# A hybrid encoder layer on one core: the B gates spread over the q, k pairs, W_c directly behind z, and one maximum tile for two heads

## The chip, the core and the metric

The kernel runs on one core of one Trainium2 chip. The metric is the time of one execution on the device, in microseconds (us), as the median of several runs. TensorE (PE, with its weight loads as PEld) does the products and the transposes, ScalarE (ACT) and VectorE (DVE) split the operands and do everything elementwise, GpSimd (POOL) does one addition per SSD head, and SyncE (SP) issues the loads of the weights. TensorE runs at one of two clock levels, 1.2 or 2.4 GHz, which the profile reports as a granted clock of 0.5 or 1.0.

## The reference

There are two layers (DEPTH 2) over 256 positions of width 1024, in float32. In each layer one combined projection of u = RMSNorm(x) feeds three branches and their gates:

```
u = RMSNorm(x);  proj = u @ w_in  ->  conv A | q, k, v | z | x, B, C of the SSD | dt | g_A, g_B, g_C
y_A = W_A (B * conv3(C * x_A))
y_B = W_B (dilated attention of q, k, v: 16 heads of 64, softmax over a mask of counts)
y_C = W_C (GroupRMSNorm((SSD_fwd + SSD_bwd + D x) * silu(z)))     4 groups of 512 channels
x = x + W_o (sig(g_A) y_A + sig(g_B) y_B + sig(g_C) y_C)
x = x + W_2 relu(W_1 RMSNorm(x))^2
```

Behind the second layer stands a final RMSNorm. What matters here: y_B needs all 16 heads, y_C needs z, the SSD output and the mean square of each group of 512 channels, and a gate needs only u.

## The kernel before, in words

Every product is done in three float32r matmuls: each operand is split into a high part and a rest (`split_to`, L172: a cast on ACT at L173, a subtraction on DVE at L174), and high by high, high by rest and rest by high are added in PSUM. I call these three matmuls a triplet. The weights come as tiles of 128 x 1024 in the order in which they are used (`Stream`, L150; the order is `_weight_stream`, L886). The raw tile has 4 buffers, its two parts `wh` and `wl` have 3 each.

Two forms of product occur. `chunks` (L189) gives the output with channels on the partitions: a weight tile is 8 triplets of 256 columns, and a q, k pair is two such tiles (L181 to L184). `wide` (L229) gives the output with positions on the partitions: one weight tile is 4 triplets of 512 columns, done as two steps of 2 triplets, one for each half of the positions (t = 0, 1), with two PSUM banks open until its last step (L248 to L250). With `lag=1`, as for W_c, the second half runs one tile behind the first. There are 4 PSUM banks for products (`mm`), two for scores (`s`), one for transposes (`pt`) and one for attention and SSD outputs (`oy`).

Two things set the order. TensorE's program is written out: `Slots` counts ticks, one for every 4 triplets of `chunks` and for every step of `wide`, and a job that was launched with a delay places its own matmuls when its tick comes. The other engines' programs are ordered at build time by a scheduler from priorities; at run time each engine goes through its own list in order and waits where an operand isn't there.

Around the change a layer goes: gate A, W_a, then eight q, k pairs (L694 to L702), gate B with its eight weight tiles (L711), the wait for all attention (L713), W_b, four groups of z (L734 to L744) with a `group_norm` job each (L720), gate C (L745), a wait for the fourth group's norm (L747), W_c (L779), W_o.

- `attention` (L638) is launched 5 ticks after its pair, for two heads. It places four score matmuls (tile `s`, L644); DVE adds the mask and takes maxima (L653), scales them (L655), ACT does the exponentials (L657) with sums, DVE the reciprocals (L659), ACT the scaling (L661, tile `scr`). Five ticks after the scores come the transposes of the first head (tile `pt`, L668), two ticks later those of the second, then the product with v (L682).
- `ssd_pair` (L520) does two SSD heads: sums on POOL (L531) and DVE (L532), exponentials on ACT (L534, L538), two DVE products (L542, L543), then the output matmuls (L552). `ssd_job` (L559) holds new pairs back between the first q, k pair and the sixth attention.
- `group_norm` waits GN_DELAY ticks behind its group of z, sums squares over channels with a matmul (tile `sqa`, L288), waits GN_DELAY2 ticks, spreads the factor over the partitions with another matmul (tile `pt`, from `rs`, L303), and scales and splits four channel tiles (L730, then L173 and L174 to `ch` and `cl`). The fourth group has a raised priority.
- A tile that takes 8 KB of a partition (`big`, L137) has one of 11 buffers; a twelfth waits until one is free.

Of the kernel before, what the change touches and what calls it, by code (L numbers as in the profile page):

```python
# [11 lines left out]
F32 = mybir.dt.float32  # L12
# [6 lines left out]
P = 128  # L19
# [25 lines left out]
Y_DELAY = 6  # L45
SSD_RESUME = 5
SSD_START = 4
GN_DELAY = 9, 9
GN_DELAY2 = 6, 5


def _bits(v, n):
# [36 lines left out]
def trunk_kernel(ctx: ExitStack, tc: tile.TileContext, xT, pos, wst, wdt, small, fin, consts, out):  # L89
# [136 lines left out]
                    tick()  # L226
        return ps

    def wide(st, r, sink, lag=0):  # L229

        rows = sum(h.shape[1] for h, _ in r)
        per = r[0][0].shape[1]
        for c in range(2):
            ps = [mmbank(), mmbank()]
            n = rows // 2
            ws = {}
            order = [(i, t) for i in range(n) for t in range(2)]
            for i, t in sorted(order, key=lambda a: (a[0] + lag * a[1], a[1])):  # L240
                if t == 0:
                    ws[i] = [t_.rearrange("p (k c) -> p k c", k=2) for t_ in st.next()]
                wh, wl = ws[i] if t == 0 else ws.pop(i)
                us = slice(t * 128, t * 128 + 128)
                for k in range(2):
                    kt = 2 * i + k
                    rh, rl = (t_[:, kt % per, us] for t_ in r[kt // per])
                    PE.matmul(ps[t], rh, wh[:, k, :], start=kt == 0, stop=False)  # L248
                    PE.matmul(ps[t], rh, wl[:, k, :], start=False, stop=False)  # L249
                    PE.matmul(ps[t], rl, wh[:, k, :], start=False, stop=kt == rows - 1)  # L250
                if i == n - 1:
                    sink(t, c, ps[t])
                tick()

    def half(tile_, t, c):

        v_ = tile_.rearrange("p a b -> p (a b)").rearrange("p (t c) -> p t c", t=2)
        return v_[:, t, c * 512 : c * 512 + 512]
# [129 lines left out]
    def layer(l, xw, squares):  # L388
# [131 lines left out]
        def ssd_pair(g, hp, xt, cb, ar, crs):  # L520
            bs = ssd["bs"]
            ct = 4 * g + hp
            av = []
            for j in range(2):
                h = 2 * ct + j
# [98 lines left out]
        mix = big("mix", F32)  # L624

        def gate(dst):
            wide(st, [u], lambda t, c, ps: ACT.activation(half(dst, t, c), ps, AF.Tanh, scale=0.5))

        ga = big("ga", F32)
        gate(ga)  # L630
        wide(st, [(ah, al)], lambda t, c, ps: DVE.scalar_tensor_tensor(
            half(mix, t, c), half(ga, t, c), 1.0, ps, ALU.add, ALU.mult))
        bh, bl = big("bh"), big("bl")
# [4 lines left out]
        def attention(c, qk):  # L638
            scs, prts = [], []
            sps = [bank("s", 2), bank("s", 2)]  # L640
            for t in range(2):
                for j in range(2):
                    rows = slice(j * 64, j * 64 + 64)
                    PE.matmul(sps[j][:, t * 256 : t * 256 + 256], qk[rows, 0, t * 128 : t * 128 + 128],  # L644
                              qk[rows, 1, :], start=True, stop=True)
            for j, sp in enumerate(sps):
                sc = scr[:, (2 * c + j) % 4]
                scs.append(sc)
                mx = tmp.tile([P, 2], F32, name="mx", bufs=4)
                den = tmp.tile([P, 2], F32, name="den", bufs=4)  # L650
                rden = tmp.tile([P, 2], F32, name="rden", bufs=4)
                for t in range(2):
                    DVE.tensor_tensor_reduce(sc[:, t, :], sp[:, t * 256 : t * 256 + 256], cntm[:, t, :],  # L653
                                             1.0, -3.0e38, ALU.add, ALU.max, mx[:, t : t + 1])
                DVE.tensor_scalar(mx, mx, -0.125, None, ALU.mult)  # L655
                for t in range(2):
                    ACT.activation(sc[:, t, :], sc[:, t, :], AF.Exp, bias=mx[:, t : t + 1], scale=0.125,  # L657
                                   accum_out=den[:, t : t + 1])
                DVE.reciprocal(rden, den)  # L659
                for t in range(2):  # L660
                    ACT.activation(sc[:, t, :], sc[:, t, :], AF.Copy, scale=rden[:, t : t + 1])  # L661
            yield 2
            yield 3
            for j in range(2):
# [26 lines left out]
        done.add("qk")  # L691
        cosb = cosT.unsqueeze(1).to_broadcast([P, 2, 256])
        sinb = sinT.unsqueeze(1).to_broadcast([P, 2, 256])
        for c in range(8):  # L694
            psv = chunks(st, 2, u)
            qk = tmp.tile([P, 2, 256], F32, name="qk", bufs=2)
# [3 lines left out]
            DVE.tensor_tensor(sw, sw, sinb, ALU.mult)  # L700
            DVE.tensor_tensor(qk, qk, sw, ALU.add)
            slots.launch(attention(c, qk), ATT_DELAY)  # L702

        def gated_add(g_):
            def sink(t, c, ps):
# [2 lines left out]
                DVE.tensor_tensor(m, m, th, ALU.add)  # L708
            return sink

        gb = big("gb", F32)  # L711
        gate(gb)
        slots.until(lambda: "attention" in done)  # L713
        wide(st, [(bh, bl)], gated_add(gb))

# [18 lines left out]
        for g in range(4):  # L734
# [7 lines left out]
                DVE.tensor_tensor(xq, xq, sz, ALU.mult)  # L742
                sq.add(xq)
            slots.launch(group_norm(g, xg, sq), GN_DELAY[g == 3])  # L744
        gc = big("gc", F32)  # L745
        gate(gc)
        slots.until(lambda: ("norm", 3) in done)  # L747

        mh, ml = big("mh"), big("ml")
        mixv = mix.rearrange("p a b -> p (a b)").rearrange("p (t c) -> p t c", t=2)  # L750
# [25 lines left out]
            if t == 1 and c == 0:  # L776
                slots.launch(turn_job(0), 6)

        wide(st, [(ch[0], cl[0]), (ch[1], cl[1])], c_sink, 1)  # L779


        xm = Pairs("xm", 2)
# [103 lines left out]
def _weight_stream(w_in, w_a, w_b, w_c, w_o, w1, w2, last):  # L886
    seq = []
# [5 lines left out]
    for g in range(4):  # L893
        seq += [xb[16 + g], xb[20 + g], ab[2 * g], ab[2 * g + 1]]
        seq += [xb[4 * g], xb[4 * g + 1], ab[8 + 2 * g], ab[9 + 2 * g]]
        seq += [xb[4 * g + 2], xb[4 * g + 3], ab[16 + 2 * g], ab[17 + 2 * g]]
    seq += _wide(w_in[:, og : og + 1024]) + _wide(w_a)
    for c in range(8):
        seq += [inb[oq][c], inb[oq][8 + c]]
    seq += _wide(w_in[:, og + 1024 : og + 2048]) + _wide(w_b)  # L900
    seq += list(inb[oz]) + _wide(w_in[:, og + 2048 : og + 3072]) + _wide(w_c)
    for w in (w_o, w1) + (() if last else (w2,)):
        wb = _blocks(w)
        for c in range(wb.shape[0]):
# [85 lines left out]
```

## Time and profile before

| | us |
|---|---|
| median of 3 runs (1377.03, 1384.38, 1382.09) | 1382.09 |
| the profiled execution's own time | 1378.66 |
| its span from first to last instruction | 1376.9 |
| PE busy in the span | 1351.1 (98%) |
| DVE busy | 1034.3 (75%) |
| ACT busy | 877.0 (64%) |
| mean granted clock of TensorE | 0.998 |

Busy time is a sum over the span. Matmuls are pipelined, so that the starts of two in a row, not their durations, tell how fast TensorE goes. The last column of a wait is the longest single one. Of one layer's stretches only the ones that the change touches are shown below; the second layer repeats the first some 680 us later.

### The profile page before, as it was taken

The numbers are of one execution on the slowest core, as the hardware profiler recorded it, in microseconds if no ns is written. First come the engines' busy times: TensorE is split into PE (matmuls) and PEld (weight loads), VectorE is DVE, ScalarE is ACT, GpSimd is POOL, SyncE is SP. The second block draws the span as 40 slices with busy tenths as digits, with TensorE's granted clock in tenths as the row PEclk, the third lists the DMA queues.
The fourth block names the chain that finished last, engine by engine and source line by source line (L and its number), as shares of the span: only waits on it lengthen the run. The fifth ranks groups of instructions, "written<-read, shape, count | busy, mean of one in ns | idle before, by whom it ended". The sixth has DMA issues, their size and how long they took to land.

```text
span 1376.9 us, 22642 instructions
## 1 busy us (share of the span) xinstructions
PE 1351.1 (98%) x8628; PEld 1186.5 (86%) x8628; DVE 1034.3 (75%) x1686; ACT 877.0 (64%) x1459; POOL 73.3 (5%) x73
## 2 busy tenths in 40 slices
PE   7999999999999999999999999999999999999997
PEld 5999987887798898888889999788778988988886
DVE  7887899984867577866578878999757766777554
ACT  6757687787577455554556586778875764655443
POOL 0000033100000000000000001331010000000000
PEclk9999999999999999999999999999999999999999
DMA  7565566534444555555544655664344455555453
GB/s 259 174 215 182 189 209 214 176 132 138 167 171 169 192 183 186 188 191 191 186 167 170 218 184 181 227 211 160 123 153 166 172 172 194 188 188 188 172 194 112
DMA packets 73693, 249.62 MB, mean 181 GB/s; under 512 B 8241, under 2 KB 8497, under 8 KB 73585
## 3 DMA queue, kind: packets, MB, share of 16 engines
q1 hardware_dynamic: 63696, 230.00, 48.3%
q10 hardware_dynamic: 9648, 17.42, 4.0%
q8 instruction: 67, 1.10, 0.3%
q0 software_dynamic: 240, 0.77, 0.2%
q14 instruction: 42, 0.34, 0.1%
HBM read 246.97 MB, written 1.18 MB: 180 GB/s over the span
## 4 chain that ended last, share of the span: by engine, by line
PE 89%; DVE 6%; ACT 3%; issue 1%; DMA 1%; SPq 0%; ACTq 0%
PE mm L222 13%; PE mm L248 11%; PE mm L181 11%; PE mm L183 11%; PE mm L184 11%; PE mm L249 10%; PE mm L250 10%; PE mm L223 6%; PE oy L552 2%; DVE wl L174 2%; ACT wh L173 1%; PE oy L682 1%; PE pt L668 1%; PE pt L571 1%; PE s L578 1%
## 5 line engine op out<-in xcount | busy, mean ns | idle before, releaser
L174 DVE TENSOR_TENSOR wl<-raw,wh 128x1024 fp32r<-128x1024 f32 (+1 forms) x436 | 534.6, 1227 | 274.9 <-ACT wh L173 268.7
L173 ACT CAST wh<-raw 128x1024 fp32r<-128x1024 f32 (+1 forms) x436 | 455.5, 1045 | 426.3 <-PE mm L250 152.9
L181 PE MATMUL mm<-uh,wh 128*128 128x256 f32 x1296 | 372.0, 287 | 0.0
L183 PE MATMUL mm<-ul,wh 128*128 128x256 f32 x1296 | 366.6, 283 | 0.0
L184 PE MATMUL mm<-uh,wl 128*128 128x256 f32 x1296 | 366.5, 283 | 0.0
L181 PEld LDWEIGHTS mm<-uh,wh 128*128 128x128 f32 x1296 | 248.3, 192 | 9.6 <-issue 9.4
L183 PEld LDWEIGHTS mm<-ul,wh 128*128 128x128 f32 x1296 | 248.5, 192 | 0.2
L184 PEld LDWEIGHTS mm<-uh,wl 128*128 128x128 f32 x1296 | 248.4, 192 | 0.0
L222 PE MATMUL mm<-xm,wh 128*128 128x512 f32 x512 | 180.0, 396 | 0.5 <-DVE xm L312 0.5
L223 PE MATMUL mm<-xm,wl 128*128 128x256 f32 x512 | 143.5, 280 | 0.0
L531 POOL TENSOR_TENSOR lg<-cr,cst 128x256 f32<-128x256 f32 x64 | 71.1, 1121 | 957.9 <-ACT xs L506 669.0
L222 PEld LDWEIGHTS mm<-xm,wh 128*128 128x128 f32 x512 | 96.0, 188 | 23.4 <-DVE xm L312 1.1
L223 PEld LDWEIGHTS mm<-xm,wl 128*128 128x128 f32 x512 | 96.7, 189 | 0.0
L222 PE MATMUL mm<-sr,wh 128*128 128x512 f32 x256 | 88.8, 391 | 0.0
L248 PE MATMUL mm<-wh,uh 128*128 128x512 f32 x192 | 79.5, 414 | 0.0
L249 PE MATMUL mm<-wl,uh 128*128 128x512 f32 x192 | 75.2, 392 | 0.0
L250 PE MATMUL mm<-wh,ul 128*128 128x512 f32 x192 | 75.0, 391 | 0.0
L223 PE MATMUL mm<-sr,wl 128*128 128x256 f32 x256 | 71.7, 280 | 0.0
L538 ACT ACTIVATE ar<-cr,bs 128x256 f32<-128x256 f32 x128 | 58.7, 501 | 1.5 <-PE oy L552 1.4
L222 PEld LDWEIGHTS mm<-sr,wh 128*128 128x128 f32 x256 | 47.9, 187 | 10.5
L504 DVE SCALAR_TENSOR_TENSOR cacc<-xs,sm,cacc 128x254 f32<-128x254 f32 (+1 forms) x128 | 53.7, 476 | 0.1
L248 PE MATMUL mm<-wh,sr 128*128 128x512 f32 x128 | 50.2, 392 | 0.0
(215 smaller groups left out, 2248.8 us busy)
## 6 DMA issues: line engine op xcount, KB each, us to landing
raw<-in_wst_dram SPq DMA_DIRECT2D x432, 512.0 KB, 3.7
cr<-cumd ACTq DMA_DIRECT2D x64, 256.0 KB, 4.1
x<-in_xT_dram SPq DMA_DIRECT2D x4, 256.0 KB, 6.6
raw<-in_wdt_dram SPq DMA_DIRECT2D x2, 512.0 KB, 4.0
cst<-in_consts_dram SPq DMA_DIRECT2D x1, 706.0 KB, 8.3
finw<-in_fin_dram POOLq DMA_DIRECT2D x1, 512.0 KB, 6.2
out_dram<-xtok ACTq DMA_DIRECT2D x2, 256.0 KB, 2.5
out_dram<-xtok SPq DMA_DIRECT2D x2, 256.0 KB, 2.5
```

What stands on the lines that cost most here:

```text
L173: ACT.copy(dst_h, src)
L174: DVE.tensor_tensor(dst_l, src, dst_h.bitcast(F32), ALU.subtract)
L181: PE.matmul(ps, wh[:, kt, :], rh[:, kt, :], start=first and kt == kts[0], stop=False, skip_group_check=True)
L183: PE.matmul(ps, wh[:, kt, :], rl[:, kt, :], start=False, stop=False, skip_group_check=True)
L184: PE.matmul(ps, wl[:, kt, :], rh[:, kt, :], start=False, stop=last and kt == kts[-1], skip_group_check=True)
L222: PE.matmul(ps, wh[:, k, :], r.both(kt), start=kt == 0, stop=False, skip_group_check=True)
L223: PE.matmul(ps[:, 0:256], wl[:, k, :], r.part(kt, 0)[:, 0, :], start=False, stop=kt == 8 * kbs - 1, skip_group_check=True)
L248: PE.matmul(ps[t], rh, wh[:, k, :], start=kt == 0, stop=False)
L249: PE.matmul(ps[t], rh, wl[:, k, :], start=False, stop=False)
L250: PE.matmul(ps[t], rl, wh[:, k, :], start=False, stop=kt == rows - 1)
L531: POOL.tensor_tensor(lg, cr[:, 0::3, :], msk, ALU.add)
L538: ACT.activation(a[:, t * 256 : t * 256 + 256], cr[:, 2 - 2 * t : 4 - 2 * t, :].rearrange("p t l -> p (t l)"), AF.Exp, bias=bs[:, t, 32 * ...
```

## The change

The eight weight tiles of gate B are taken one at a time, each directly behind a q, k pair. Gate C, with its weights, moves from behind z to directly behind these. W_b follows, then z, and W_c stands directly behind z; in place of one wait for the fourth norm it asks before each step that the group which the step reads has placed its norm (`need`). To that end the fourth norm's delays are shortened from 9 and 5 ticks to 6 and 4. In the attention the maxima, sums and reciprocals of two heads share one tile of 4 columns, so that one scaling and one reciprocal serve both heads. An SSD pair is held back until the pair three before it has placed its output.

```diff
-GN_DELAY = 9, 9
-GN_DELAY2 = 6, 5
+GN_DELAY = 9, 6
+GN_DELAY2 = 6, 4
...
-    def wide(st, r, sink, lag=0):
+    def wide_steps(st, r, sink, lag=0, need=None):
...
             for i, t in sorted(order, key=lambda a: (a[0] + lag * a[1], a[1])):
+                if need:
+                    need(i)
...
                 tick()
+                if t == 1:
+                    yield
+
+    def wide(*a, **k):
+        for _ in wide_steps(*a, **k):
+            pass
...
             ct = 4 * g + hp
+            while ct >= 3 and ("y", ct - 3) not in done:
+                yield 1
...
+            mx = tmp.tile([P, 2, 2], F32, name="mx", bufs=2)
+            den = tmp.tile([P, 2, 2], F32, name="den", bufs=2)
+            rden = tmp.tile([P, 2, 2], F32, name="rden", bufs=2)
             for j, sp in enumerate(sps):
...
                 for t in range(2):
                     DVE.tensor_tensor_reduce(sc[:, t, :], sp[:, t * 256 : t * 256 + 256], cntm[:, t, :],
-                                             1.0, -3.0e38, ALU.add, ALU.max, mx[:, t : t + 1])
-                DVE.tensor_scalar(mx, mx, -0.125, None, ALU.mult)
+                                             1.0, -3.0e38, ALU.add, ALU.max, mx[:, j, t : t + 1])
+            DVE.tensor_scalar(mx, mx, -0.125, None, ALU.mult)
+            for j, sc in enumerate(scs):
                 for t in range(2):
-                    ACT.activation(sc[:, t, :], sc[:, t, :], AF.Exp, bias=mx[:, t : t + 1], scale=0.125,
-                                   accum_out=den[:, t : t + 1])
-                DVE.reciprocal(rden, den)
+                    ACT.activation(sc[:, t, :], sc[:, t, :], AF.Exp, bias=mx[:, j, t : t + 1], scale=0.125,
+                                   accum_out=den[:, j, t : t + 1])
+            DVE.reciprocal(rden, den)
+            for j, sc in enumerate(scs):
                 for t in range(2):
-                    ACT.activation(sc[:, t, :], sc[:, t, :], AF.Copy, scale=rden[:, t : t + 1])
+                    ACT.activation(sc[:, t, :], sc[:, t, :], AF.Copy, scale=rden[:, j, t : t + 1])
...
+        gb = big("gb", F32)
+        gate_b = gate(gb)
         for c in range(8):
...
             slots.launch(attention(c, qk), ATT_DELAY)
+            next(gate_b)
...
-        gb = big("gb", F32)
-        gate(gb)
+        assert next(gate_b, "end") == "end"
+        gc = big("gc", F32)
+        list(gate(gc))
         slots.until(lambda: "attention" in done)
...
-        gc = big("gc", F32)
-        gate(gc)
-        slots.until(lambda: ("norm", 3) in done)
...
-        wide(st, [(ch[0], cl[0]), (ch[1], cl[1])], c_sink, 1)
+        wide(st, [(ch[0], cl[0]), (ch[1], cl[1])], c_sink, 1,
+             need=lambda i: slots.until(lambda: ("norm", i // 2) in done))
...
     for c in range(8):
-        seq += [inb[oq][c], inb[oq][8 + c]]
-    seq += _wide(w_in[:, og + 1024 : og + 2048]) + _wide(w_b)
-    seq += list(inb[oz]) + _wide(w_in[:, og + 2048 : og + 3072]) + _wide(w_c)
+        seq += [inb[oq][c], inb[oq][8 + c], gb[c]]
+    seq += gc + _wide(w_b) + list(inb[oz]) + _wide(w_c)
```

How the programs of three engines stand at three places, before and after. Line numbers of the changed file are larger by 9 to 16: its L543, L553 and L554 are L532, L542 and L543 of before, its L665, L667 and L672 are L653, L655 and L659, its L714 to L717 are L698 to L701, its L251 to L253 are L248 to L250, its L302 and L312 are L293 and L303.

First, DVE in the first layer at the first attention, from the maxima of its scores to its first reciprocal (`qk` and `sw` belong to the next q, k pair, `ar`, `lg` and `cb` to the SSD, `wl` is the rest of a weight tile), before:

```order
L653 ISA mx 128x1
L701 TENSOR_TENSOR qk<-qk,sw 128x512
L653 ISA scr,mx<-s,cst 128x256
L653 ISA mx 128x1
L653 ISA scr,mx<-s,cst 128x256
L653 ISA mx 128x1
L655 TENSOR_SCALAR mx<-mx 128x2
L653 ISA scr,mx<-s,cst 128x256
L653 ISA mx 128x1
L543 TENSOR_TENSOR ar<-ar,cb 128x512
L174 TENSOR_TENSOR wl<-raw,wh 128x1024
L659 RECIPROCAL rden<-den 128x2
```

And now:

```order
L665 ISA scr,mx<-s,cst 128x256
L665 ISA mx 128x1
L554 TENSOR_TENSOR ar<-ar,cb 128x512
L667 TENSOR_SCALAR mx<-mx 128x4
L714 TENSOR_TENSOR qk<-mm,cosT 128x512
L715 STREAM_SHUFFLE sw<-mm 128x512
L174 TENSOR_TENSOR wl<-raw,wh 128x1024
L716 TENSOR_TENSOR sw<-sw,sinT 128x512
L553 TENSOR_TENSOR ar<-ar,lg 128x2x128
L717 TENSOR_TENSOR qk<-qk,sw 128x512
L174 TENSOR_TENSOR wl<-raw,wh 128x1024
L672 RECIPROCAL rden<-den 128x4
```

Between the scaled maxima and the reciprocal stood two maxima's rows, one SSD product and one split of a weight; now seven instructions of other jobs stand there: the four of the second q, k pair, an SSD sum and two splits.

Second, PE in the first layer at the matmuls that spread the third group's norm factor (`rs` into `pt`), before; `uh` is u, the two `mm` are gate C's banks:

```order
L250 MATMUL mm_4803<-wh_4869,ul_128 128x512
L303 MATMUL pt_4880<-cst_78,rs_4822 128x128 x2
L248 MATMUL mm_4804<-wh_4869,uh_127 128x512
L249 MATMUL mm_4804<-wl_4870,uh_127 128x512
L250 MATMUL mm_4804<-wh_4869,ul_128 128x512
```

And now; `ch0` holds groups one and two, `ch1` groups three and four, the `mm` are W_c's banks:

```order
L253 MATMUL mm_4918<-wh_4959,cl0_4335 128x512
L312 MATMUL pt_5001<-cst_78,rs_4936 128x128 x2
L251 MATMUL mm_4917<-wh_5018,ch1_4334 128x512
L252 MATMUL mm_4917<-wl_5019,ch1_4334 128x512
L253 MATMUL mm_4917<-wh_5018,cl1_4336 128x512
```

Behind the spreading matmuls stood products that need only u; now the next one reads the first channel tile that is scaled by their result. The fourth group's spreading matmuls stand three steps later, and one step lies between them and the first product that reads that group.

Third, ACT in the first layer from the third group's square root to the last cast of the fourth group's channel tiles (`ch`), before:

```order
L293 ACTIVATE ms<-pt,epsc 128x2
L173 CAST wh<-raw 128x1024
L277 ACTIVATE sq<-xs_387 128x512
L173 CAST wh<-raw 128x1024 x2
L627 ACT_TABLE_LOAD
L627 ACTIVATE gc<-mm 128x512
L173 CAST wh<-raw 128x1024
L173 CAST ch_4215<-xs_387 128x256 x2
L293 ACT_TABLE_LOAD
L293 ACTIVATE ms<-pt,epsc 128x2
```

And now:

```order
L302 ACTIVATE ms<-pt,epsc 128x2
L286 ACTIVATE sq<-xs_387 128x512
L173 CAST wh<-raw 128x1024 x2
L302 ACTIVATE ms<-pt,epsc 128x2
L173 CAST wh<-raw 128x1024
L173 CAST ch_4334<-xs_387 128x256 x4
L173 CAST wh<-raw 128x1024
L173 CAST ch_4334<-xs_387 128x256
L173 CAST wh<-raw 128x1024
L173 CAST ch_4334<-xs_387 128x256 x3
```

The tanh of gate C and its table loads are gone from here. The four casts of the third group stand together, and a weight's cast stands in front of them, another in front of the fourth group's first cast and a third between that one and the other three.

## Rows read from the trace of the kernel before

**Rows 1.** Waits of PE, whole run: us in total, times, longest.

```profile
PE pt L668 <- ACT prt L673: 5.7, 6, 1.4
PE pt L288 <- DVE sqa L285: 3.3, 2, 2.2
```

**Rows 2.** Busy time by stretch: start:end, length, then us busy (instructions) per engine, PEclk, DMA.

```profile
70.00:120.00 50.00, 50.00 (x420) 50.00 (x419) 43.74 (x77) 29.34 (x44) 0.00 (x0) 1.00 0.61 204
244.00:295.00 51.00, 48.22 (x381) 42.33 (x381) 48.97 (x129) 42.31 (x108) 6.54 (x7) 1.00 0.48 161
917.00:975.00 58.00, 55.03 (x437) 48.57 (x436) 55.93 (x137) 47.27 (x119) 9.54 (x10) 1.00 0.49 164
```

**Rows 3.** Timeline of PE, first layer, first attention: start, us, instruction, [idle before].

```profile
249.79 1.14 PE L644 MATMUL s<-qk 64*128 64x256 f32 x8
...
259.41 0.69 PE L668 MATMUL pt<-cst,scr 128*128 128x128 f32 x4
...
264.35 0.66 PE L668 MATMUL pt<-cst,scr 128*128 128x128 f32 x4 [1.39 <-ACT prt L673]
```

**Rows 4.** Timeline of DVE, same place.

```profile
243.61 0.68 DVE L698 TENSOR_TENSOR qk<-mm,cosT 128x512 f32<-128x512 f32 x1
...
248.66 0.46 DVE L556 SCALAR_TENSOR_TENSOR xs<-xs,sm,oy 128x256 f32<-128x256 f32 x1
...
250.15 0.68 DVE L698 TENSOR_TENSOR qk<-mm,cosT 128x512 f32<-128x512 f32 x1
...
253.67 0.41 DVE L653 CUSTOM_DVE_ANT_0 scr<-s,cst 128x256 f32<-128x256 f32 x1
...
255.30 0.16 DVE L655 TENSOR_SCALAR mx<-mx 128x2 f32<-128x2 f32 x1
255.37 0.41 DVE L653 CUSTOM_DVE_ANT_0 scr<-s,cst 128x256 f32<-128x256 f32 x1
...
255.72 0.68 DVE L543 TENSOR_TENSOR ar<-ar,cb 128x512 f32<-128x512 f32 x1
256.32 1.21 DVE L174 TENSOR_TENSOR wl<-raw,wh 128x1024 fp32r<-128x1024 f32 x1
257.46 0.15 DVE L659 RECIPROCAL rden<-den 128x2 f32<-128x2 f32 x1
```

**Rows 5.** Timeline of ACT, same place.

```profile
257.64 0.51 ACT L661 ACTIVATE scr<-scr,rden 128x256 f32<-128x256 f32 x1 [1.05 <-DVE rden L659]
258.06 1.03 ACT L173 CAST wh<-raw 128x1024 fp32r<-128x1024 f32 x1
258.99 0.51 ACT L661 ACTIVATE scr<-scr,rden 128x256 f32<-128x256 f32 x1
```

**Rows 6.** Busy time by stretch, columns as in rows 2: an attention wait, the layer boundary.

```profile
262.00:264.00 2.00, 0.96 (x9) 0.76 (x7) 1.89 (x10) 2.00 (x5) 0.00 (x0) 1.00 0.68 231
692.00:694.00 2.00, 0.10 (x1) 0.10 (x1) 1.81 (x4) 0.11 (x1) 0.00 (x0) 1.00 0.36 135
694.00:696.00 2.00, 2.00 (x8) 1.71 (x9) 0.17 (x1) 0.26 (x1) 0.00 (x0) 0.60 0.64 227
696.00:698.00 2.00, 2.00 (x6) 1.56 (x6) 0.00 (x0) 0.65 (x1) 0.00 (x0) 0.55 0.00 0
```

**Rows 7.** Timeline of PE, first layer, gate C: third and fourth group's spreading matmuls.

```profile
425.01 0.39 PE L248 MATMUL mm<-wh,uh 128*128 128x512 f32 x1
425.69 0.61 PE L303 MATMUL pt<-cst,rs 128*128 128x128 f32 x4
426.05 0.48 PE L248 MATMUL mm<-wh,uh 128*128 128x512 f32 x1
...
436.19 0.61 PE L303 MATMUL pt<-cst,rs 128*128 128x128 f32 x4
```

**Rows 8.** Timeline of DVE, same place: the third and the fourth group's first rests.

```profile
429.95 0.75 DVE L174 TENSOR_TENSOR cl<-xs,ch 128x256 fp32r<-128x256 f32 x2
...
438.02 0.76 DVE L174 TENSOR_TENSOR cl<-xs,ch 128x256 fp32r<-128x256 f32 x2
```

More of the change, by code (lines that the diff above doesn't have):

```diff
@@ L626, in gate @@
         def gate(dst):
-            wide(st, [u], lambda t, c, ps: ACT.activation(half(dst, t, c), ps, AF.Tanh, scale=0.5))
+            return wide_steps(st, [u],
+                              lambda t, c, ps: ACT.activation(half(dst, t, c), ps, AF.Tanh, scale=0.5))
         ga = big("ga", F32)
-        gate(ga)
+        list(gate(ga))
         wide(st, [(ah, al)], lambda t, c, ps: DVE.scalar_tensor_tensor(
@@ L648, in attention @@
                 scs.append(sc)
-                mx = tmp.tile([P, 2], F32, name="mx", bufs=4)
-                den = tmp.tile([P, 2], F32, name="den", bufs=4)
-                rden = tmp.tile([P, 2], F32, name="rden", bufs=4)
                 for t in range(2):
                     DVE.tensor_tensor_reduce(sc[:, t, :], sp[:, t * 256 : t * 256 + 256], cntm[:, t, :],
-                                             1.0, -3.0e38, ALU.add, ALU.max, mx[:, t : t + 1])
-                DVE.tensor_scalar(mx, mx, -0.125, None, ALU.mult)
+                                             1.0, -3.0e38, ALU.add, ALU.max, mx[:, j, t : t + 1])
+            DVE.tensor_scalar(mx, mx, -0.125, None, ALU.mult)
+            for j, sc in enumerate(scs):
                 for t in range(2):
-                    ACT.activation(sc[:, t, :], sc[:, t, :], AF.Exp, bias=mx[:, t : t + 1], scale=0.125,
-                                   accum_out=den[:, t : t + 1])
-                DVE.reciprocal(rden, den)
+                    ACT.activation(sc[:, t, :], sc[:, t, :], AF.Exp, bias=mx[:, j, t : t + 1], scale=0.125,
+                                   accum_out=den[:, j, t : t + 1])
+            DVE.reciprocal(rden, den)
+            for j, sc in enumerate(scs):
                 for t in range(2):
-                    ACT.activation(sc[:, t, :], sc[:, t, :], AF.Copy, scale=rden[:, t : t + 1])
+                    ACT.activation(sc[:, t, :], sc[:, t, :], AF.Copy, scale=rden[:, j, t : t + 1])
             yield 2
@@ L897, in _weight_stream @@
     seq += _wide(w_in[:, og : og + 1024]) + _wide(w_a)
+    gb, gc = (_wide(w_in[:, og + o : og + o + 1024]) for o in (1024, 2048))
     for c in range(8):
-        seq += [inb[oq][c], inb[oq][8 + c]]
-    seq += _wide(w_in[:, og + 1024 : og + 2048]) + _wide(w_b)
-    seq += list(inb[oz]) + _wide(w_in[:, og + 2048 : og + 3072]) + _wide(w_c)
+        seq += [inb[oq][c], inb[oq][8 + c], gb[c]]
+    seq += gc + _wide(w_b) + list(inb[oz]) + _wide(w_c)
     for w in (w_o, w1) + (() if last else (w2,)):
```

## The prediction

> **What bounds the kernel now.** I read the waits of PE first, then busy time by stretch, then the timelines at the two places that the change rebuilds. In a stretch without attention 420 matmuls start in 50.00 us and PE is never idle [rows 2]: a triplet of 256 columns takes 3 x 0.119 = 0.36 us, and one of 512 columns 0.68 us (425.01 to 425.69) [rows 7]. No weight or activation that comes earlier can shorten that. What can be won is PE's idle time, and the waits of PE name little of it: six for the copy of an attention's transposes, 5.7 us in all, and two of up to 2.2 us at the norm on a layer's edge [rows 1], which the change doesn't touch. The stretches agree: PE is busy 48.22 of 51.00 us and 55.03 of 58.00 us while the q, k pairs run, and DVE is busy 48.97 and 55.93 us there [rows 2]. So 2.78 + 2.97 = 5.75 us are idle, because DVE and ACT can't follow. That is 0.4% of the run, and it is the ceiling of what the change can gain; a new wait of PE counts in full against it.
>
> **The change part by part.**
>
> *B gates between the pairs.* A gate step takes 4 x 0.68 = 2.7 us of PE and one weight for DVE and ACT, against 16 x 0.36 = 5.8 us and two weights for a q, k pair. PE then stays some 2.7 us longer at each pair, while DVE gets only one split of 1.14 us (256.32 to 257.46) [rows 4] on top. From the second attention on, that takes away what made PE wait: -5.75 us. The matmuls and the weight loads are as many as before, so nothing else changes on PE.
>
> *The first attention, with the shared maxima.* Here the gain is given back. Before, 20 triplets and the next pair's scores stand between the first scores (249.79) and the first transposes (259.41) [rows 3]: 20 x 0.36 + 2 x 1.1 = 9.4 us, and the second copy that they need started at 258.99 [rows 5]; it came just in time. Now 12 triplets, one gate step and no second set of scores stand between them: 12 x 0.36 + 2.7 + 1.1 = 8.1 us, and the scores come 0.2 us earlier, at 249.6, since a gate step replaces 8 triplets in front of them as well. PE asks for the first transposes at 257.7.
>
> DVE's list is the same as before up to the row at 250.15 [rows 4], and it runs without a pause there. From that row the new order has an SSD sum, a product, a split, two sums of 256 columns, four maxima, a product, the scaling: 0.35 + 0.60 + 1.14 + 2 x 0.35 + 4 x 0.35 + 0.60 + 0.07 = 4.86 us by the starts from 255.30 to 257.46 [rows 4]. I take every sum of 256 columns as long as a maximum. Then come seven instructions of others before the reciprocal. The same seven in a row (the four of a q, k pair, an SSD sum, two splits) took 243.61 to 248.66, 5.05 us [rows 4]. The reciprocal starts at 250.15 + 4.86 + 5.05 = 260.06, where the first head's stood at 257.46 [rows 4]. The first copy started 0.18 us behind it and 0.42 us before its follower [rows 5], so that two are done at about 261.1. PE waits 261.1 - 257.7 = 3.4 us. POOL's additions can slow DVE on the way; I take 4.0 us a layer. Below, the old chain needed 259.41 - 249.79 = 9.6 us and is offered 8.1, and merging two heads can't shorten it for the first: 1.4 us. Above, I allow 5. Behind this wait DVE has caught up, and the later attentions find their copies ready. Two layers: +8.0 us (2.8 to 10).
>
> Of the merged tile the trace says that a scaling of two columns holds DVE from 255.30 to 255.37 [rows 4], 0.07 us; 16 such instructions fewer in a layer are 1.1 us of DVE. The Trainium skill (Perfetto Trace Analysis, Optimizing Scalar/DVE Operations) says that grouping into larger operations helps where the engine is saturated, and that breaking instructions up helps where the engine isn't saturated but makes another one wait. By its first half the sum would be 2 x 1.1 us better; by its second half, which fits the first attention, where one head alone would be ready sooner, nothing is won. I go by the second and count nothing.
>
> *The clock.* At the layer's edge PE was busy for 0.10 us between 692 and 694 us, and then the granted clock was 0.60 and 0.55 for two stretches of 2 us; in the attention's wait, 0.96 us busy between 262 and 264, it stayed 1.00 [rows 6]. The first drop cost 2 x 0.40 + 2 x 0.45 = 1.7 us. An empty stretch of 4 us looks like the first case: +1.7 us a layer, +3.4 us (0 to 6.8, if W_c's waits do it too).
>
> *W_c directly behind z.* Before, the third group's spreading matmuls (425.69) and the fourth's (436.19) stood among gate C's products [rows 7], which hid what follows. What follows is long: the first rest of the third group's channels starts on DVE at 429.95, 4.26 us later, and that of the fourth, with its raised priority, at 438.02, 1.83 us later [rows 8]. A rest takes some 0.38 us (two in 0.75 [rows 8]). Now the third group's spreading matmuls are followed at once by a triplet that reads the first channel tile: its third matmul wants the rest after 0.36 us (425.69 to 426.05 [rows 7]) plus 0.45 us. PE waits between 1.83 + 0.38 - 0.81 = 1.4 us and 4.26 + 0.38 - 0.81 = 3.8 us. In the new order gate C's tanh and table loads are gone from ACT, so the casts come nearer to the short case, but on DVE a weight's split of 1.14 us still stands in front of the first rest: 2.2 us. The fourth group has one step of 1.36 us in between. By its own old row it would cost 1.83 + 0.38 - 0.81 - 1.36, below nothing, so 0; by the third group's row 2.5 us. Here ACT has a weight's cast in front of the last three channel casts, and that cast needs a buffer that the step in between gives free: I take 1.65 us, some two thirds of the way. Together 3.85 us a layer, +7.7 us (2.8 to 12.6). Moving gate C itself costs nothing: its products are the same.
>
> *The rest.* The twelfth large tile (gate C) waits for the score tile's buffer; its first banks are wanted again only after 32 triplets x 0.68 / 2, 11 us later, and without that cover it would cost a wait of a gate step, 2.7 us. The new brake on SSD pairs delays only SSD outputs, and none of these stands among the waits of PE [rows 1]: nothing, or one gate step again if it did.
>
> **The sum.** -5.75 + 8.0 + 3.4 + 7.7 = +13.35 us, on 1378.66 us of the profiled execution: 1392.0. That execution stands 3.4 us below the median of the three runs, whose spread is 7.4; I add 1: **1393 us**. With all costs at their low ends it is -0.15 us, with all at their high ends +23.65.
>
> **The rivals.**
>
> *A. Only W_c waits.* If the first attention's copies come in time, 8.0 and 3.4 us go: +1.95 us, 1381. For it speaks that ACT and DVE keep their later lists and that I have added up a list of 20 instructions; against it the seven strangers in front of the reciprocal.
>
> *B. The interleaving wins.* PE waits nowhere: -5.75 us, 1373 to 1376, not slower. The mechanism is the one that the change has for it: one weight more on DVE for 2.7 us more of PE in each pair. It decides if neither the first attention nor the norms are late. Against it speaks 1.83 us, the shortest way from spreading to rest, with 0.81 us to hide it. The Trainium skill (Perfetto Trace Analysis, Optimization Strategy) says that stretches with different limits may gain by being interleaved, which is this rival; the trace bears it out for DVE in the pairs, and caps it.
>
> *C. The clock stays up.* The wait at the first attention is there without the drop: 1388.6 + 1.
>
> *D. The norms are late by the old third group's row.* 12.6 in place of 7.7 us, and the clock falls at W_c as well, +3.4: 1401. It decides if the weight casts on ACT, which wait for buffers that a waiting PE doesn't give back, hold up the channel casts.
>
> **How the numbers follow.** My forecast has 0.50 (1389 to 1398 as its own range), A 0.18, B 0.10, C 0.12, D 0.10. A median of this kernel can't be told from no change within 0.5%, 6.9 us: 1375.2 to 1389.0. Slower takes the forecast, D and some of C: 0.62. Same takes A, the rest of C and some of B: 0.31. Faster is left 0.07, part of B. The range from 1375 to 1402 leaves out the best of B and the worst of D.
>
> **What would show it.** In the waits of PE: a wait at the first transposes (`pt` of `cst`, `scr`) for ACT's `scr` of 3 to 5 us in each layer, none of the old waits for `prt`; waits of the products of `ch` and `cl` of about 4 us a layer, which before has not at all; a granted clock near 0.5 for some 3 us behind the first. If the first transposes show no wait, my DVE list is wrong; if `ch` shows none, the split chain is faster than any row of before.

## The result, and the profile after

The changed kernel takes **1399.46 us** (median of 6 runs, 1395.85 to 1403.5), the kernel before 1381.46 us in the same comparison: ratio 1.0144, 95% interval 1.0124 to 1.0163. That is 18 us slower; forecast were 1393 us, with 1375 to 1402 as the range. The profiled execution of after has a span of 1401.7 us (before 1376.9), PE busy 1363.1 us (97%) and a mean granted clock of 0.991 (before 0.998).

The waits of PE after, whole run (us in total, times, longest; left out is the 7 us wait for the first weight at the kernel's start, which both kernels have):

```profile
PE pt L682 <- ACT scr L675: 9.2, 2, 5.0
...
PE pt L297 <- DVE sqa L294: 3.3, 2, 2.2
PE oy L563 <- DVE bl L700: 2.7, 2, 1.8
PE mm L251 <- ACT ch L173: 2.6, 4, 1.0
PE mm L253 <- DVE cl L174: 2.5, 4, 0.7
```

The six waits for an attention's copy [rows 1] are gone, and the norm at the layer's edge waits as before. New are the first line (the first attention of each layer, 4.17 and 5.04 us), the third (an SSD product that runs beside gate C, 1.85 and 0.82 us) and the last two (W_c).

Now DVE behind the first attention's last maximum, first layer, to be held against [rows 4]:

```profile
255.47 0.15 DVE L667 TENSOR_SCALAR mx<-mx 128x4 f32<-128x4 f32 x1
255.54 0.68 DVE L714 TENSOR_TENSOR qk<-mm,cosT 128x512 f32<-128x512 f32 x1
...
256.78 1.21 DVE L174 TENSOR_TENSOR wl<-raw,wh 128x1024 fp32r<-128x1024 f32 x1
257.90 1.23 DVE L716 TENSOR_TENSOR sw<-sw,sinT 128x512 f32<-128x512 f32 x1
...
259.99 1.76 DVE L174 TENSOR_TENSOR wl<-raw,wh 128x1024 fp32r<-128x1024 f32 x1
261.67 0.17 DVE L672 RECIPROCAL rden<-den 128x4 f32<-128x4 f32 x1
```

The order is the forecast one: the scaling at 255.47, seven strangers, the reciprocal. These seven took 6.1 us (255.54 to 261.67) instead of the 5.05 assumed, because a product took 1.23 us and a split 1.76 us, so the reciprocal starts at 261.67 and not at 260.06. The clock behind the wait, in the first layer and at its end in the second (start:end, length, busy of PE, PEld, DVE, ACT, POOL; the third number from the right is the granted clock):

```profile
260.00:262.00 2.00, 0.00 (x0) 0.00 (x0) 2.00 (x4) 0.92 (x2) 0.66 (x1) 0.77 0.36 139
262.00:264.00 2.00, 1.57 (x7) 1.35 (x8) 2.00 (x4) 1.81 (x5) 0.00 (x0) 0.50 0.55 158
264.00:266.00 2.00, 2.00 (x11) 2.00 (x10) 1.59 (x5) 1.96 (x5) 0.00 (x0) 0.50 0.56 199
266.00:268.00 2.00, 2.00 (x10) 1.19 (x8) 0.75 (x2) 0.98 (x3) 0.00 (x0) 0.53 0.78 242
...
962.00:964.00 2.00, 2.00 (x9) 1.18 (x10) 0.41 (x2) 0.88 (x3) 0.00 (x0) 0.50 0.88 232
```

PE works for 5.5 and 6.3 us at 1.2 GHz, so 2.7 and 3.1 us are lost there, against the 1.7 us of the layer's edge [rows 6]. W_c in the first layer, on PE (the spreading matmuls, then the first products of the third and the fourth group):

```profile
453.71 0.61 PE L312 MATMUL pt<-cst,rs 128*128 128x128 f32 x4
455.36 0.50 PE L251 MATMUL mm<-wh,ch 128*128 128x512 f32 x1 [1.04 <-ACT ch L173]
456.75 0.50 PE L253 MATMUL mm<-wh,cl 128*128 128x512 f32 x1 [0.66 <-DVE cl L174]
...
464.01 0.50 PE L251 MATMUL mm<-wh,ch 128*128 128x512 f32 x1 [0.22 <-ACT ch L173]
465.30 0.50 PE L253 MATMUL mm<-wh,cl 128*128 128x512 f32 x1 [0.56 <-DVE cl L174]
```

The gaps in PE's starts are a little longer than the waits: 1.29 + 0.83 + 0.25 us at the third group (2.2 forecast) and 0.49 + 0.72 at the fourth (1.65 forecast). The unforeseen wait of the SSD product stands on DVE's order too; first DVE, then PE:

```profile
364.85 1.76 DVE L174 TENSOR_TENSOR wl<-raw,wh 128x1024 fp32r<-128x1024 f32 x1
366.54 0.41 DVE L700 TENSOR_TENSOR bl<-oy,bh 128x256 fp32r<-128x256 f32 x1
```

```profile
367.00 0.87 PE L563 MATMUL oy<-ar,xt 128*64 128x256 f32 x6 [1.85 <-DVE bl L700]
```

The only `oy` bank still holds the last attention's output until `bl` is taken from it, and `bl` stands behind a weight's split.

### The profile page after: what moved, and what is told of

It is laid out like the page before. It is cut to its first block, busy times and chain, and to the rows that moved or that the text cites. A ratio compares the mean times of both kernels' runs of the same rounds, so it can differ in the third digit from the quotient of the medians.

```text
span 1401.7 us, 22624 instructions
## 1 busy us (share of the span) xinstructions
PE 1363.1 (97%) x8628; PEld 1191.7 (85%) x8628; DVE 1038.9 (74%) x1654; ACT 866.2 (62%) x1451; POOL 77.5 (6%) x73
## 4 chain that ended last, share of the span: by engine, by line
PE 91%; DVE 5%; DMA 2%; ACT 2%; issue 1%; SPq 0%; ACTq 0%; DVEq 0%
PE mm L222 13%; PE mm L181 12%; PE mm L183 12%; PE mm L184 12%; PE mm L251 10%; PE mm L253 10%; PE mm L252 10%; PE mm L223 6%; DVE wl L174 2%; PE oy L563 2%; DMA cr<-cumd 1%; PE s L656 1%; PE pt L682 1%; PE oy L696 1%; ACT wh L173 1%
## 5 line engine op out<-in xcount | busy, mean ns | idle before, releaser
L542 POOL TENSOR_TENSOR lg<-cr,cst 128x256 f32<-128x256 f32 x64 | 75.4, 1187 | 984.0 <-ACT xs L515 666.3
L251 PE MATMUL mm<-wh,uh 128*128 128x512 f32 x192 | 79.7, 415 | 0.0
L253 PE MATMUL mm<-wh,ul 128*128 128x512 f32 x192 | 75.2, 391 | 0.0
L222 PEld LDWEIGHTS mm<-sr,wh 128*128 128x128 f32 x256 | 48.2, 188 | 11.9
L251 PE MATMUL mm<-wh,ch 128*128 128x512 f32 x128 | 52.1, 407 | 2.7 <-ACT ch L173 2.6
```

Source lines behind the costliest of these rows:

```text
L222: PE.matmul(ps, wh[:, k, :], r.both(kt), start=kt == 0, stop=False, skip_group_check=True)
L542: POOL.tensor_tensor(lg, cr[:, 0::3, :], msk, ALU.add)
```

## The experiments

Each was compared with the kernel before on the same chip; the median of before in the three sets was 1380.81, 1379.32 and 1377.35 us.

| run | what is in it | median us | ratio to before, 95% |
|---|---|---|---|
| x_nomerge | all but the shared tile | 1391.15 | 1.0073 (1.0052 to 1.0094) |
| x_gcback | gate C and W_c as before | 1405.39 | 1.0173 (1.0148 to 1.0198) |
| x_onlyB | gate B spread alone | 1390.02 | 1.0062 (1.0040 to 1.0084) |
| x_onlymerge | shared tile alone | 1380.69 | 0.9998 (0.9983 to 1.0014) |
| x_onlyC | W_c behind z alone | 1391.12 | 1.0092 (1.0077 to 1.0108) |
| x_nobrake | all but the SSD brake | 1400.12 | 1.0154 (1.0133 to 1.0175) |
| x_first | shared tile from attention 1 on | 1379.13 | 1.0002 (0.9986 to 1.0018) |
| x_best | same, priorities and one tick later | 1382.72 | 1.0026 (1.0012 to 1.0040) |
| x_fill | all, and the first wait filled | 1401.79 | 1.0158 (1.0124 to 1.0192) |
| x_half | half of gate B spread | 1382.96 | 1.0026 (1.0002 to 1.0051) |

**x_nomerge**

```diff
-            mx = tmp.tile([P, 2, 2], F32, name="mx", bufs=2)
+                mx = tmp.tile([P, 2], F32, name="mx", bufs=4)
```

(`den` and `rden` likewise, scaling and reciprocal inside the loop over heads.)

> The changed kernel with a tile of maxima, sums and reciprocals for each head again; the order of the weights stays as changed. Theory (the shared tile makes the first attention late, by the place of the reciprocal in DVE's order): with a tile for each head only about 2.4 us of DVE's list stand between the first head's scaling and its reciprocal, in place of 5.05 us. PE's wait at the first transposes (4.17 and 5.04 us) falls to 1 to 2 us in each layer, and the low clock behind it goes. 9.2 - 3 = 6.2 us of wait and some 6.4 us of clock less: 1399.5 - 12.6 = 1387 us; W_c's waits stay (3.4 us a layer). Rival (the shortened cover alone makes it late, the tile is innocent): waits of 4 to 5 us and the low clock stay, 1397 to 1400 us.

DVE around the first reciprocals, and the waits for `scr` and `prt` in the whole run:

```profile
255.35 0.16 DVE L667 TENSOR_SCALAR mx<-mx 128x2 f32<-128x2 f32 x1
...
256.67 1.20 DVE L174 TENSOR_TENSOR wl<-raw,wh 128x1024 fp32r<-128x1024 f32 x1
257.79 0.22 DVE L671 RECIPROCAL rden<-den 128x2 f32<-128x2 f32 x2
```

```profile
PE pt L680 <- ACT scr L673: 2.2, 3, 0.9
...
PE oy L694 <- ACT prt L685: 0.4, 1, 0.4
```

The reciprocals come at 257.79, 3.9 us earlier than after, PE waits 0.91 and 0.85 us at the first transposes, and the granted clock stays 1.00 there. The median is 8.3 us below that of after, against 12.6 us expected; the profiled execution is 12.1 and 10.0 us below the two profiled ones of after. In the changed order of weights the shared tile makes the first attention late; the shorter cover by itself costs no more than the 0.9 us that is left.

**x_onlymerge** (the shared tile on the old order of weights)

```diff
-                mx = tmp.tile([P, 2], F32, name="mx", bufs=4)
+            mx = tmp.tile([P, 2, 2], F32, name="mx", bufs=2)
```

> Only the shared tile of maxima, sums and reciprocals on the kernel before; all weights in the old order. Theory (the shared tile puts one reciprocal behind both heads and behind the other work in DVE's order): the first attention's copies, which came just in time, come 3 to 5 us later, so PE waits 2 to 4 us there in each layer, with some 2 to 3 us of low clock behind it, and the later pairs wait longer as well: 1381.5 + 8 = 1390 us or more. Rival (the tile only saves 16 short instructions of DVE in a layer, 0.07 us each): 1379 to 1382 us, with the waits of PE as before.

```profile
PE pt L680 <- ACT scr L673: 4.9, 2, 2.5
```

Neither: the first attention waits 2.51 and 2.41 us (1.39 and 1.27 us stood at the second transposes before), the clock falls behind it (0.50 and 0.71 between 264 and 268 us), and all six old waits are gone, without gate B spread. In the profile the stretch from the first scores to the end of W_c grows by 1.0 and 0.9 us, and 1.6 us come back at the layer's edge, where in this execution the clock didn't fall; the median doesn't move (0.9998). So the spread gate isn't the only thing that ends the old waits.

**x_onlyB** (to the kernel before, the spread gate alone)

```diff
             slots.launch(attention(c, qk), ATT_DELAY)
+            next(gate_b)
...
-        seq += [inb[oq][c], inb[oq][8 + c]]
+        seq += [inb[oq][c], inb[oq][8 + c], gb[c]]
```

> Only the first part of the change: gate B's blocks behind the q, k pairs. No shared tile, gate C where it was, no brake on the SSD pairs. Theory: the six waits for an attention's copies go (-5.75 us), and the first attention waits 1 to 2 us in each layer without a low clock behind it (+2 to +4): 1381.5 - 3 = 1378.5 us, at most within 0.5% of before. Rival (the spread gate itself costs: the first attention waits 4 us and the clock falls): 1381.5 - 5.75 + 8 + 6 = 1390 us.

It is 9 us slower, the rival's time without its reason: the first attention waits 0 and 0.76 us, the old waits are gone and the clock doesn't fall there. PE is idle elsewhere, between the last pair and W_b (326 to 341 us):

```profile
332.00:334.00 2.00, 0.90 (x6) 0.55 (x8) 0.53 (x2) 1.87 (x7) 0.00 (x0) 1.00 0.00 0
334.00:336.00 2.00, 1.86 (x12) 0.83 (x12) 0.55 (x2) 1.99 (x5) 0.00 (x0) 1.00 0.03 8
336.00:338.00 2.00, 1.28 (x8) 1.07 (x8) 0.84 (x2) 2.00 (x5) 0.00 (x0) 1.00 0.00 0
```

ACT is full there and PE has only the last attentions and SSD pairs. Gate B, whole, had been the cover for this end. From the first scores to the end of W_c the layers take 2.2 and 2.6 us longer than before, the gain of the old waits already taken off. The rest is told under the repeats.

**x_gcback**

```diff
-    seq += gc + _wide(w_b) + list(inb[oz]) + _wide(w_c)
+    seq += _wide(w_b) + list(inb[oz]) + gc + _wide(w_c)
```

(The code of gate C moves with it, one wait for the fourth norm, old delays.)

> The changed kernel with gate C between z and W_c again, as in the kernel before, with one wait for the last group norm and the old delays of the norms; gate B stays spread, the tile stays shared. Theory: the waits of the products of ch and cl go (3.4 us a layer, 6.8 us), and with them the low clock at the second layer's W_c (1.7 us); the first attention's waits and their low clock stay: 1399.5 - 8.5 = 1391 us. Rival 1 (W_c behind z is nearly all of the loss): 1381 us or less. Rival 2 (gate C in front of W_b was a cover for the end of the attentions, and W_b now waits for them): 1396 us or more, with a new wait at W_b's start.

Rival 2 held: 6 us slower than after although W_c's waits are gone. PE at the last attentions:

```profile
337.72 1.82 PE L696 MATMUL oy<-prt,v 128*64 128x256 f32 x8
342.24 1.17 PE L682 MATMUL pt<-cst,scr 128*128 128x128 f32 x4 [2.70 <-ACT scr L675]
```

With gate B spread, something else must stand in front of W_b. Moving gate C there is no free edit but the cover for the end of the attentions, and taking it away from in front of W_c is what exposes W_c.

**x_onlyC** (gate B whole as before, then gate C; W_c behind z with `need` and the new delays)

```diff
-    seq += gb + _wide(w_b) + list(inb[oz]) + gc + _wide(w_c)
+    seq += gb + gc + _wide(w_b) + list(inb[oz]) + _wide(w_c)
```

> Only the last part of the change: W_c straight behind z, waiting for each group norm by itself, with the new delays of the norms; gate B whole, then gate C, then W_b; a tile for each head, no brake on the SSD pairs. Theory (W_c's waits stand by themselves and cost what they cost in the changed kernel): waits of the products of ch and cl of 2.5 us and 1 us of restarts in each layer, and a low clock of some 3.4 us behind them in at least one layer (1.7 us); the six waits for an attention's copies stay as in the kernel before. 1381 + 7 + 1.7 = 1389.5 us. Rival (the norms are late only because the spread gate B holds up the SSD part): no wait there, 1380 to 1382 us.

```profile
PE pt L678 <- ACT prt L683: 5.1, 6, 1.4
...
PE mm L251 <- ACT ch L173: 2.6, 4, 1.0
PE mm L253 <- DVE cl L174: 2.5, 4, 0.7
```

W_c's waits are those of after to a tenth, so they don't depend on the spread gate. The clock falls behind them in the first layer (0.50 and 0.67 over 4 us) and not in the second. The 11.8 us are more than the 8.5 expected; the first MLP product has the long period here (below), 3.3 us.

**x_nobrake**

```diff
-            while ct >= 3 and ("y", ct - 3) not in done:
-                yield 1
```

> The changed kernel without the brake on the SSD pairs, all else as changed. Theory (the brake moves SSD products behind the attentions, and so makes PE wait for ar and xt at the end of gate C, 1.85 and 0.82 us): these waits go, 3 us less, 1396.5 us. Rival (these waits come from DVE's order behind the last attention, not from the brake): they stay, 1399 us.

The wait for `bl` stays, at 0.81 and 0.74 us, 0.5 to 1.1 us less in all than in the two profiles of after, and 1400.12 us is no gain: the rival held for the most part. What goes are the short waits for `ar` and `xs` ahead of the first scores (1.0 us in the profile of after). The wait at the first transposes is shorter too, 3.1 and 3.7 us; so in this profile the brake has a share in it, which the median does not show.

**x_first** (the shared tile on the old order, but a tile for each head in attention 0)

```diff
+            one = c == 0
+            n = 1 if one else 2
+            for k in range(0, 2, n):
+                mx = tmp.tile([P, n, 2], F32, name="mx" + tag, bufs=2)
```

> The kernel before with the shared tile for attentions 1 to 7 and a tile for each head in attention 0. Theory (the shared tile ends the waits of the later pairs, 0.56 + 0.83 + 0.58 + 1.12 = 3.1 us in the two layers, and costs only at the first attention, which comes first in a list of DVE that is full): the first attention's waits are those of before, 1.39 and 1.27 us, the later ones gone, no low clock behind them: 1380.8 - 3.1 = 1377.7 us. Rival (the later waits went because the first one gave DVE time): they come back, 1381 us.

```profile
PE pt L674 <- ACT scr L667: 3.0, 2, 1.8
PE pt L674 <- ACT prt L679: 2.6, 2, 1.4
```

The rival held, in another place: now the second attention, the first with a shared tile, waits 1.21 and 1.75 us for `scr`. The sum of both lines is 5.6 us, as much as before; DVE is busy for 20.00 of 20 us from 240 and 19.84 of 20 us from 260 us. The wait goes where the list is longest.

**x_best** (to x_first; a priority around the scaling, and likewise around the reciprocal)

```diff
+                with tc.high_priority(offset=PRIO_W):
                     DVE.tensor_scalar(mx, mx, -0.125, None, ALU.mult)
...
-            yield 3
+            yield 4 if one else 3
```

> As the kernel with the shared tile for attentions 1 to 7 only, and besides the scalings and reciprocals in front of weight splits in DVE's order, and the first attention's transposes one step of four triplets (1.44 us) later. Theory: none of the six waits is left, -5.75 us: 1375 us (1373 to 1377), the ceiling of what the change could win. Rival (the later transposes or the moved splits make another product wait): 1378 to 1382 us, with a new wait for wl or at W_b.

Waits of 8.1 us for `scr` and `prt` in place of 5.7, and the scores themselves come 1.3 us later in each layer, behind SSD products that wait for `ar` and `xs`. On this full engine, what was put first put another thing last.

**x_half** (to x_onlyB; the order of the weights follows)

```diff
-            next(gate_b)
+            if c < 4:
+                next(gate_b)
...
+        list(gate_b)
```

> Gate B in two parts: four blocks behind the q, k pairs 0 to 3, where DVE is full, and four between the last pair and W_b, where the last attentions and SSD pairs run out; a tile for each head, gate C between z and W_c, no brake, the old delays. Theory (the spread blocks end the waits for an attention's copies, and the whole spread failed because nothing was left to cover the end of the attentions): no waits there beyond 0.8 us in a layer, none at W_b's start, -4 us: 1380 - 4 = 1376 us, plus up to 3.4 us where the first MLP product runs with the longer period. Rival (W_b's start still waits with four blocks of cover): 1382 us or more, with waits for scr and prt ahead of W_b.

Not faster: waits of 4.0 us for `prt` and 2.5 us for `scr`, of which 2.0 us in each layer behind the eighth pair, where ACT is busy for 9 of 10 us. No order here beats the kernel before.

**x_fill**

```diff
+                if c == 0 and j == 0:
+                    for _ in range(38):
+                        PE.matmul(tp[:, 0:256], uh[:, 0, 0:128], uh[:, 1, :], start=True, stop=True)
```

> The changed kernel with 38 matmuls of 256 columns, whose result nobody reads, in front of the first attention's transposes in each layer (38 x 0.119 = 4.5 us); all else as changed. They fill the wait there and change nothing of what is waited for. Theory (a second cost of that wait is the low clock behind it, 3.4 us lost in each layer): the named wait falls below 1 us, the granted clock stays 1.00 there, and 2 x 3.4 = 6.8 us go: 1399.5 - 6.8 = 1393 us (1391 to 1395). Rival (the low clock is only a sign, and DVE and ACT set the pace behind the wait): 1398 to 1400 us.

The clock did stay at 1.00 at both first attentions, and the time did not fall. PE there in x_fill, in after and in the second execution of after (after_again, below); products left out:

```profile
258.17 4.72 PE L682 MATMUL pt<-uh 128*128 128x256 f32 x38
263.02 0.94 PE L685 MATMUL pt<-cst,scr 128*128 128x128 f32 x4
...
267.92 0.60 PE L685 MATMUL pt<-cst,scr 128*128 128x128 f32 x4
...
274.26 1.08 PE L699 MATMUL oy<-prt,v 128*64 128x256 f32 x6 [0.99 <-ACT prt L690]
...
277.59 0.95 PE L685 MATMUL pt<-cst,scr 128*128 128x128 f32 x4 [0.62 <-ACT scr L675]
```

```profile
262.43 1.30 PE L682 MATMUL pt<-cst,scr 128*128 128x128 f32 x4 [4.17 <-ACT scr L675]
...
269.63 0.60 PE L682 MATMUL pt<-cst,scr 128*128 128x128 f32 x4
...
276.92 0.60 PE L682 MATMUL pt<-cst,scr 128*128 128x128 f32 x4
```

```profile
264.39 1.30 PE L682 MATMUL pt<-cst,scr 128*128 128x128 f32 x4 [5.07 <-ACT scr L675]
...
277.87 0.60 PE L682 MATMUL pt<-cst,scr 128*128 128x128 f32 x4
```

From the first head's transposes to the second's PE needs 4.90 us with the clock up and 7.20 us with it down: 2.3 us won. From there to the second attention's transposes it needs 9.67 us against 7.29: 2.4 us lost again, in waits for `prt` and `scr` that after does not have. The rival's time came, but not its reason. The fillers changed the order that the scheduler gives the other engines: on DVE an SSD sum now stands in front of the second attention's maxima (in after that sum comes behind them, at 273.21), and on ACT the first head's copy to `prt` stands behind other work, 2.7 us after its transposes began instead of 1.3 (first layer). DVE in x_fill:

```profile
270.34 0.42 DVE L543 TENSOR_TENSOR cr<-cr,cst 128x256 f32<-128x256 f32 x1 [2.74 <-DMA cr<-cumd]
270.68 0.42 DVE L665 CUSTOM_DVE_ANT_0 scr<-s,cst 128x256 f32<-128x256 f32 x1
```

DVE stood idle there for 2.74 us (3.43 us in the second layer) until a load had come, while the scores, placed at 265.32, waited. So x_fill changes two things at once and doesn't show what the low clock costs. Runs that keep DVE's order of after at this place and differ in the clock do show it. From the first transposes to those of the second attention:

| execution, layer | lost to the low clock | us needed | less the lost |
|---|---|---|---|
| after, first and second | 2.7, 3.1 | 14.5, 14.8 | 11.8, 11.7 |
| after again, first and second | 1.7, 1.7 | 13.5, 13.6 | 11.8, 11.9 |
| x_gcback, first and second | 1.5, 3.1 | 13.3, 14.8 | 11.8, 11.7 |

No copy is waited for in any of the six, and the time follows the clock's loss nearly one to one: here the low clock is a price of the run. The Trainium skill (TensorE: Matmul & The Clock Gate, HAM oscillation — how this bites in real kernels) prices a throttled stretch at half of its length; these rows agree with it.

**after_again, before_again**: both kernels once more, unchanged, a single run each (1401.31 and 1377.82 us).

> The changed kernel once more, for what repeats: the waits at the first transposes (4.2 and 5.0 us), their low clock (3.4 us lost in each), W_c's waits (2.5 us a layer), the wait for bl at gate C's end (1.85 and 0.82 us), and the period of the MLP's pairs of matmuls, 0.3534 us in layer 1 and 0.3467 us in layer 2. Theory (the periods are a draw of each execution): another pair of periods may come. Rival (the long period in layer 1 belongs to the changed order of the weights): 0.3534 us there again.

> The kernel before once more: the six waits for an attention's copies (5.7 us) and the period of the MLP's pairs of matmuls, 0.3467 us in layer 1 and 0.3534 us in layer 2 in the first profile. Theory (a draw of each execution): another pair of periods may come. Rival (it belongs to the kernel): the same periods.

The waits repeat: 9.7 us at the first transposes, 4.9 us at W_c, 2.1 us for `bl`; before, 4.9 us of old waits. The clock repeats less: behind the first attention 1.7 us are lost in each layer instead of 2.7 and 3.1, and at W_c, where after lost 1.7 us in its second layer, nothing. And in the MLP, where the change touches nothing, the same pair of matmuls (512 and 256 columns) starts every 0.3467 us in some stretches and every 0.3534 us in others, at a granted clock of 1.00. The high-part matmuls (x) of a first-layer and a second-layer stretch: before, after, after again:

```profile
560.00:660.00 100.00, 100.00 (x290) 53.97 (x289) 1.00 0.55 190
1230.00:1275.00 45.00, 45.00 (x129) 23.98 (x128) 1.00 0.54 186
```

```profile
560.00:660.00 100.00, 100.00 (x285) 53.22 (x284) 1.00 0.55 187
1230.00:1275.00 45.00, 45.00 (x131) 24.41 (x130) 1.00 0.57 188
```

```profile
560.00:660.00 100.00, 100.00 (x285) 53.20 (x284) 1.00 0.54 186
1230.00:1275.00 45.00, 45.00 (x128) 23.96 (x128) 1.00 0.55 187
```

A stretch keeps its period from its first product to its last. In the second layer after had the short one and after again the long one: there it is a draw. In the first layer it was long in both profiles of after and in x_nomerge, x_gcback, x_onlyB, x_onlyC, x_nobrake and x_fill, and short in both of before and in x_onlymerge, x_first, x_best and x_half. That goes with the kernel, and is worth 3.3 us of its loss; what decides it stays open, with one profile for most.

## Why the prediction was right or wrong

Time by stage in the profiles, after less before, and after again less before again: from the first scores to the end of W_c, both layers, +21.3 and +18.4 us; the first layer's W_o and MLP +3.3 and +3.3; from the kernel's and the second layer's start to their first scores +1.5 and +1.5; the second layer's end -1.3 and +0.3. These +24.8 and +23.5 us stand above the 18 us of the medians: the profiled executions of before took 1378.66 and 1377.82 us, those of after 1403.5 and 1401.31. The first stage by the prediction's terms, in us:

| term | forecast | after | after again |
|---|---|---|---|
| old attention waits | -5.75 | -5.7 | -4.9 |
| wait at the first transposes | +8.0 | +9.2 | +9.7 |
| low clock behind it | +3.4 | +5.8 | +3.4 |
| W_c, gaps of PE | +7.7 | +7.0 | +7.2 |
| low clock at W_c | 0 | +1.7 | 0 |
| SSD product behind `bl` | 0 | +2.7 | +2.1 |
| sum | +13.35 | +20.7 | +17.5 |

The old waits of the last column are those of before again. Low clock is summed as (1 - granted clock) x length where PE was busy.

- **Right: the sign, the first attention and W_c.** The wait was worked out from DVE's order, and both its cause (x_nomerge) and its size (4.0 forecast, 4.2 to 5.1 measured, the upper bound reached) hold. W_c came to 3.5 us a layer against 3.85, by the long third and the short fourth group as forecast. That one head alone would be ready sooner also holds: 0.9 us of wait in place of 4 to 5. The Trainium skill (Perfetto Trace Analysis, Optimizing Scalar/DVE Operations) advises breaking instructions up where the engine isn't saturated; the trace goes beyond it, since DVE is busy for 20.00 of the 20 us from 240 us, in after and in x_nomerge.
- **Right in the mechanism, in part luck in the size: the clock, and "Behind this wait DVE has caught up, and the later attentions find their copies ready."** In both profiles of after PE waits for no later copy. The low clock was forecast to cost 3.4 us; the first profile of after lost 5.8 and the second 3.4, behind waits of much the same length, and the table under x_fill shows that the loss is paid nearly in full. What the runs don't show is the changed kernel, in its own order, with the clock up there.
- **Wrong: the brake and the end of the attentions cost nothing.** That "none of these stands among the waits of PE" was an inference from a kernel in which gate B covered the end. The wait for `bl` is 2.1 to 2.7 us; 1.6 us of it stay without the brake (x_nobrake), so most of it comes from DVE's order. The waits for `ar` and `xs` ahead of the scores, 0.6 to 1 us, go with the brake.
- **Half right: the ceiling of 5.75 us.** The old waits went, but not for one reason: the shared tile alone ends them too. As a gain they were not to be had: in x_onlymerge, x_first, x_best and x_half waits of 4.9 to 8.1 us stand in their place. Between 240 and 280 us, in the first layer, DVE is busy for 18.5 to 20.0 of each 20 us in all four; that this is why the waits only move is argued from it, not tested.
- **"Moving gate C itself costs nothing"** held only because gate C took over gate B's cover (x_onlyB, x_gcback).
- **Not foreseen:** the long period in the first layer's MLP, 3.3 us. Of the 6.5 us between forecast and median 1.8 us are the base (1379.7 in the forecast, 1381.46 in the comparison). For the other 4.7 us the profiles offer more than is needed: this period, 2.1 to 2.7 us of the `bl` wait, 1.2 to 1.7 us of the larger first wait, and the clock. How they are shared in a median run isn't shown.

## What to carry to other kernels

Where PE waited here because another engine was full, a new order mostly moved the wait: count that engine's instructions, not PE's gaps alone, and ask for each block of products that is moved what its old place covered. A reduction shared by two consumers is ready when the later one is, plus all that the in-order engine puts between; look at the row in front of the reciprocal before merging. And an experiment that adds work to one engine can reorder the others: compare their lists before reading the time. Here the idle matmuls that held the clock up brought a wait for a load in front of the maxima, and only executions with the same order told what the low clock costs.

## What was not expected of the hardware

- After waits of 3.1 to 5.1 us the time at 1.2 GHz came in two lengths, some 3.4 and some 6.8 us, also for the same wait: 5.07 us was followed by 1.7 us lost in one execution, 5.04 us by 3.1 us in another. A wait of 2.5 us (x_onlymerge) was followed by the short one, of 0.9 us (x_nomerge) by none. The same wait of 2.2 us at the layer's edge was followed by the short one in twelve of the fourteen profiles, by the long one in x_onlyB and by none in x_onlymerge.
- W_c's two gaps of 1.29 and 0.83 us, with two matmuls between, were followed by a low clock in some layers and not in others of the same kernel.
- The same two matmuls, back to back at a granted clock of 1.00, repeat in 0.3467 or 0.3534 us for 180 us on end, 1.9% apart.
